# A decoder layer on one core: the first four products of each tile as high, high, low, low

## The chip, the core and the metric

The kernel runs on one core of a Trainium2 chip. Its time is device microseconds of one execution. Before the change it takes 1614.85 us, the median of three runs (1614.5 to 1615.77).

## The reference

One layer of a decoder with 256 tokens and 2048 features, all in float32. A combined projection of the normalised input gives the merge gates and the heads of three token mixers (sparse attention over compressed, selected and recent blocks; stick-breaking attention; attention over keys that an indexer selects). Their outputs are projected, gated, summed and projected once more; then come a gated feed-forward network with a short causal convolution, and a per-layer embedding behind a sigmoid gate. Cut to what matters here:

```python
h = rmsnorm(x, norm_mix)
u = h @ w_in                                  # gates and heads of the three mixers
y = g0 * (o_a @ w_a) + g1 * (o_b @ w_b) + g2 * (o_c @ w_c)
x = x + y @ w_out
h = rmsnorm(x, norm_ffn)
x = x + (gelu(conv(h @ w_gate) + conv_b) * (h @ w_up)) @ w_down
x = x + sigmoid(rmsnorm(x, norm_ple) @ ple_w_gate) * (p @ ple_w_proj)
return rmsnorm(x, norm_final)
```

## The kernel before

Activations are kept with features on the partitions and the 256 tokens along the free dimension. Each float32 operand is split in two rounded parts: a high part, rounded to TensorE's fast float32 format, and a low part, what the rounding left. An activation tile `xs[k]` has 128 features and 512 columns: the high parts of the 256 tokens, then the low parts. A weight block is split in the same way by `split_w` (L114): ScalarE copies the high part (L122), VectorE subtracts it for the low part (L123).

A tile of a matrix product is one block of 128 output features in one PSUM bank of 512 columns. `gemm` (L134) loops over the blocks k of 128 input features. For each it issues two products: the high weights times all 512 columns of `xs[k]` (L140, "a high product"), which leaves high times high in the left half of the bank and high times low in the right half; and the low weights times the 256 high columns alone (L141, "a low product"), added in the right half. `fold` or `add_x` then adds the two halves. Each product loads its own 128 by 128 weights.

`gemm` is called for the feature tiles of the combined projection (35, four of them early, in four pieces of four blocks while the input still arrives), for 48 gate tiles, 48 projections of the mixers (4, 4 or 8 blocks of input), 16 output tiles, 88 tiles of gate and up, and 64 of down (11 blocks). All others have 16 blocks. The weights of a tile come in one or two parts (`parts`), split one after the other; `k0` and `total` say where a piece stands in its tile.

`tile_of` (L216) loads and splits the weights of a tile one tile ahead of the products that use them: the products wait in `pending` until the next tile's load is issued. Attention's small products (`stick`, `index`, `selected`, `sparse`) are generators that `pump` advances by one step between tiles. The value tiles (L328 to L330) and the embedding's gate (L818 to L820) issue their products in threes with other operands, and do not call `gemm`.

The order in which an engine runs its instructions is not quite that of the code. A planner with a simulated timeline orders them when the program is built (`schedule_with_timeline_sim`, L1068), and may put a later instruction ahead of an earlier one that it expects to wait.

Of the kernel before, what the change touches and what calls it, by code (L numbers as in the profile page):

```python
# [38 lines left out]
def trunk(ctx, tc, xT, xtok, pT, wf, wv, wg, wpa, wpb, wpc, wout, ck1, cv1, gmix, params, fg, fu, fd,  # L39
# [12 lines left out]
    mm = nc.tensor.matmul  # L52
# [12 lines left out]
    def feat(name, dt=F32):  # L65
        return f2.tile([P, 512], dt, tag="f2", name=name)
# [18 lines left out]
    for g in range(4):  # L85
        for c in range(2):
            k = 4 * g + 2 * c
# [46 lines left out]
    def gemm(ps, parts, xs, k0=0, total=None):  # L134
        total = total or sum(n for _, _, n in parts)
        k = k0
        for hi, lo, n in parts:
            for j in range(n):
                last = k == total - 1
                mm(ps[:, 0:512], hi[:, j, :], xs[k][:, 0:512], start=k == 0, stop=last)  # L140
                mm(ps[:, 256:512], lo[:, j, :], xs[k][:, 0:256], start=False, stop=last, skip_group_check=True)  # L141
                k += 1

    def fold(dst, ps, name):
        t = tmp("fold")
# [84 lines left out]
    for g in range(4):  # L230
        raw = early_raw[g].rearrange("p (k c) -> p k c", c=128)
        parts = []
        for c in range(2):
            for k in range(4 * g + 2 * c, 4 * g + 2 * c + 2):
                xs = feat("h", F32R)
                act(xs[:, 0:256], x_sb[:, k, :], AF.Copy, scale=gm[:, k:k + 1])
                vec.scalar_tensor_tensor(xs[:, 256:512], x_sb[:, k, :], gm[:, k:k + 1], xs[:, 0:256].bitcast(F32),
                                         op0=ALU.mult, op1=ALU.subtract)
                hs.append(xs)
            parts += split_w(raw[:, 8 * c:8 * c + 8, :], (4, 4) if g == 0 else (8,), 128, g == 0)  # L240
        if g:
            parts = [(hi[:, a:a + 4, :], lo[:, a:a + 4, :], 4) for hi, lo, _ in parts for a in (0, 4)]
        for n in range(EARLY):
            gemm(ps_early[n], parts[n:n + 1], hs, 4 * g, KT)
# [30 lines left out]
    def feature_tiles(n, name, into=None):  # L275
# [27 lines left out]
        def load(parts, i):  # L303
            ps = psg()
            gemm(ps, parts, hs)
            evac(i, ps)
# [368 lines left out]
    def gate_tile(parts):  # L675
        ps = psg()
        gemm(ps, parts, hs)
        gt = tmp("gt")
        fold_norm(gt, ps, norm[0])
        act(gt, gt, AF.Tanh, scale=0.5)  # L680
        latent["gt"] = gt
        pump()
# [58 lines left out]
    xs = []  # L741
# [333 lines left out]
```

## Time and profile before

| what | before |
|---|---|
| median of three runs | 1614.85 us |
| profiled execution | 1616.5 us |
| its span | 1614.7 us |
| PE busy | 1602.2 us (99%) |
| weight loads (PEld) busy | 1403.1 us (87%) |
| VectorE busy | 1136.6 us (70%) |
| ScalarE busy | 869.6 us (54%) |
| HBM traffic over the span | 195 GB/s |

The span is what the profiler saw between the first and the last instruction; the execution's own time is 1.8 us longer. PE is TensorE's matrix product, PEld its weight loads, which overlap the products. A product's duration in a row includes the time until its results are out, and the next product starts before that; so the distance between two starts says what a product costs.

### The profile page before, as it was taken

To read this page: it belongs to the slowest core of one execution; us is meant where nothing else is said; L and a number is where in the kernel's file an instruction comes from. 1 tells how busy PE (TensorE), PEld (TensorE's weight loads), DVE (VectorE), ACT (ScalarE), POOL (GpSimd) and SP (SyncE) were. 2 spreads that over 40 slices of the span, in tenths; PEclk is the share of its full clock that TensorE was granted. 3 is DMA by queue.
4 is the path that set the end of the run, shared out by engine and by line. 5 is a ranking of instruction groups with operands and counts; after the bars stand their busy time and mean duration, and the time that the engine had idled before them with its cause. 6 is when DMAs were issued, how large, how long until landed. Compare 5 with 4: busy or idle time off the path is not lost.

```text
span 1614.7 us, 24245 instructions
## 1 busy us (share of the span) xinstructions
PE 1602.2 (99%) x9186; PEld 1403.1 (87%) x9186; DVE 1136.6 (70%) x1897; ACT 869.6 (54%) x1407; POOL 171.6 (11%) x193
## 2 busy tenths in 40 slices
PE   9999999999999999999999999999999999999997
PEld 8888888888888888888888888888888888888886
DVE  5555857777777666677777777667776677678785
ACT  6585556555555555555655555445544555446554
POOL 0201512100010100022000000000000000002442
PEclk9999999999999999999999999999999999999999
DMA  9854456444445555555555554565546655566862
GB/s 359 286 192 159 166 200 239 169 164 158 164 164 183 193 192 195 209 191 200 184 183 188 199 188 160 178 236 183 186 153 209 209 191 176 164 195 211 278 233 79
DMA packets 57933, 313.39 MB, mean 194 GB/s; under 512 B 6412, under 2 KB 8152, under 8 KB 30040
## 3 DMA queue, kind: packets, MB, share of 16 engines
q1 hardware_dynamic: 54048, 302.05, 53.7%
q0 software_dynamic: 1600, 5.24, 1.0%
q10 hardware_dynamic: 2168, 4.54, 0.9%
q8 instruction: 72, 1.18, 0.3%
q14 instruction: 45, 0.37, 0.1%
HBM read 307.53 MB, written 6.57 MB: 195 GB/s over the span
## 4 chain that ended last, share of the span: by engine, by line
PE 98%; DVE 1%; DMA 0%; ACT 0%; issue 0%; SPq 0%; POOLq 0%; DVEq 0%; ACTq 0%
PE pg L140 56%; PE pg L141 29%; PE pg L818 1%; PE pg L820 1%; PE pg L819 1%; PE pa L820 1%; PE pa L818 1%; PE pa L819 1%; PE pg L329 1%; PE pg L330 1%; PE pg L328 1%; PE po L632 1%; PE po L541 0%; PE po L540 0%; DMA raw<-in_wf_dram 0%; PE pa L589 0%
## 5 line engine op out<-in xcount | busy, mean ns | idle before, releaser
L123 DVE TENSOR_TENSOR lo<-raw,hi 128x1024 fp32r<-128x1024 f32 (+2 forms) x611 | 696.5, 1142 | 371.7 <-ACT hi L122 370.4
L122 ACT ACTIVATE hi<-raw 128x1024 fp32r<-128x1024 f32 (+2 forms) x611 | 598.3, 981 | 644.9 <-PE pg L140 404.9
L140 PE MATMUL pg<-xf,hi 128*128 128x512 f32 x1408 | 488.5, 391 | 0.0
L140 PE MATMUL pg<-h,hi 128*128 128x512 f32 x1300 | 462.4, 397 | 0.2 <-DVE pj L147 0.2
L141 PE MATMUL pg<-xf,lo 128*128 128x256 f32 x1408 | 394.2, 280 | 0.0
L141 PE MATMUL pg<-h,lo 128*128 128x256 f32 x1300 | 366.4, 282 | 0.0
L140 PEld LDWEIGHTS pg<-xf,hi 128*128 128x128 f32 x1408 | 263.3, 187 | 57.7
L140 PEld LDWEIGHTS pg<-h,hi 128*128 128x128 f32 x1300 | 243.6, 188 | 55.7 <-issue 0.7
L141 PEld LDWEIGHTS pg<-xf,lo 128*128 128x128 f32 x1408 | 266.1, 189 | 0.1
L141 PEld LDWEIGHTS pg<-h,lo 128*128 128x128 f32 x1300 | 245.5, 189 | 2.4 <-issue 0.4
L140 PE MATMUL pg<-f,hi 128*128 128x512 f32 x704 | 245.5, 392 | 0.0
L141 PE MATMUL pg<-f,lo 128*128 128x256 f32 x704 | 197.2, 280 | 0.0
L140 PEld LDWEIGHTS pg<-f,hi 128*128 128x128 f32 x704 | 131.7, 187 | 29.4
L141 PEld LDWEIGHTS pg<-f,lo 128*128 128x128 f32 x704 | 133.0, 189 | 0.7
L721 POOL TENSOR_TENSOR ssq<-ssq,sqn 128x256 f32<-128x256 f32 x28 | 32.2, 1151 | 794.6 <-ACT sqn L720 794.6
L140 PE MATMUL pg<-ys,hi 128*128 128x512 f32 x256 | 88.7, 393 | 0.0
L270 POOL TENSOR_TENSOR gt<-fold,r 128x256 f32<-128x256 f32 x48 | 38.3, 799 | 354.2 <-DVE fold L269 281.6
L141 PE MATMUL pg<-ys,lo 128*128 128x256 f32 x256 | 70.8, 277 | 0.0
L140 PEld LDWEIGHTS pg<-ys,hi 128*128 128x128 f32 x256 | 47.9, 187 | 11.0
L146 ACT ACTIVATE fold<-pg 128x256 f32<-128x256 f32 x141 | 51.5, 365 | 6.8 <-PE pg L141 6.8
L141 PEld LDWEIGHTS pg<-ys,lo 128*128 128x128 f32 x256 | 48.1, 188 | 0.1
L140 PE MATMUL pg<-oa,hi 128*128 128x512 f32 x128 | 45.1, 391 | 0.0
(312 smaller groups left out, 1732.2 us busy)
## 6 DMA issues: line engine op xcount, KB each, us to landing
raw<-in_wg_dram SPq DMA_DIRECT2D x48, 1024.0 KB, 4.8
raw<-in_fg_dram SPq DMA_DIRECT2D x44, 1024.0 KB, 4.8
raw<-in_fu_dram SPq DMA_DIRECT2D x44, 1024.0 KB, 4.9
raw<-in_fd_dram SPq DMA_DIRECT2D x64, 704.0 KB, 4.0
raw<-in_wf_dram SPq DMA_DIRECT2D x31, 1024.0 KB, 4.9
raw<-in_wout_dram SPq DMA_DIRECT2D x16, 1024.0 KB, 4.8
raw<-in_plg_dram SPq DMA_DIRECT2D x16, 1024.0 KB, 5.0
raw<-in_wv_dram SPq DMA_DIRECT2D x8, 1024.0 KB, 5.9
```

The source lines that it names most:

```text
L122: act(hi, raw[:, k:k + n, :], AF.Copy)
L123: vec.tensor_tensor(lo, raw[:, k:k + n, :], hi.bitcast(F32), op=ALU.subtract)
L140: mm(ps[:, 0:512], hi[:, j, :], xs[k][:, 0:512], start=k == 0, stop=last)
L141: mm(ps[:, 256:512], lo[:, j, :], xs[k][:, 0:256], start=False, stop=last, skip_group_check=True)
L146: act(t, ps[:, 256:512], AF.Copy)
L270: nc.gpsimd.tensor_tensor(dst, t, r, op=ALU.mult)
L328: mm(pss[t], xh, hi[:, j, :], start=k == 0, stop=False)
L329: mm(pss[t], xl, hi[:, j, :], start=False, stop=False)
L721: (vec if n == KT - 1 else nc.gpsimd).tensor_tensor(ssq, ssq, t, op=ALU.add)
L818: mm(ps, xh, hi, start=first, stop=False)
L819: mm(ps, xl, hi, start=False, stop=False)
L820: mm(ps, xh, lo, start=False, stop=last)
```

## The change

In a piece of a tile that starts at block 0, and only in its first part, the second and the third product change places: high 0, high 1, low 0, low 1, then in turns as before. Which products are issued, their operands and the marks of the first and the last one of a tile stay as they are.

```diff
         for hi, lo, n in parts:
-            for j in range(n):
-                last = k == total - 1
-                mm(ps[:, 0:512], hi[:, j, :], xs[k][:, 0:512], start=k == 0, stop=last)
-                mm(ps[:, 256:512], lo[:, j, :], xs[k][:, 0:256], start=False, stop=last, skip_group_check=True)
-                k += 1
+            order = [(m, j) for j in range(n) for m in (0, 1)]
+            if k == 0:
+                order[1:3] = order[2:0:-1]
+            last = k + n == total
+            for m, j in order:
+                if m == 0:
+                    mm(ps[:, 0:512], hi[:, j, :], xs[k + j][:, 0:512], start=k + j == 0, stop=last and j == n - 1)
+                else:
+                    mm(ps[:, 256:512], lo[:, j, :], xs[k + j][:, 0:256], start=False, stop=last and j == n - 1,
+                       skip_group_check=True)
+            k += n
```

## Rows read from the trace of the kernel before

**Rows 1.** The page: span, busy time of TensorE, shares of the chain that ended last.

```profile
span 1614.7 us, 24245 instructions
...
PE 1602.2 (99%) x9186; PEld 1403.1 (87%) x9186; DVE 1136.6 (70%) x1897; ACT 869.6 (54%) x1407; POOL 171.6 (11%) x193
...
PE 98%; DVE 1%; DMA 0%; ACT 0%; issue 0%; SPq 0%; POOLq 0%; DVEq 0%; ACTq 0%
```

**Rows 2.** DMA issues by tile: count, size, us to landing.

```profile
raw<-in_wg_dram SPq DMA_DIRECT2D x48, 1024.0 KB, 4.8
...
raw<-in_fd_dram SPq DMA_DIRECT2D x64, 704.0 KB, 4.0
raw<-in_wf_dram SPq DMA_DIRECT2D x31, 1024.0 KB, 4.9
```

**Rows 3.** Feed-forward network: high products in 400 us; timeline (start, duration) of neighbours.

```profile
1000.00:1400.00 400.00, 400.00 (x1155) 215.75 (x1155) 1.00 0.56 187
...
600.08 0.39 PE L140 MATMUL pg<-h,hi 128*128 128x512 f32 x1
600.31 0.28 PE L141 MATMUL pg<-h,lo 128*128 128x256 f32 x1
600.43 0.39 PE L140 MATMUL pg<-h,hi 128*128 128x512 f32 x1
```

**Rows 4.** Timeline: first and last of 55 products of 512, then 34 of 256.

```profile
1540.12 0.39 PE L818 MATMUL pa<-hi,xp 128*128 128x512 f32 x1
...
1552.36 0.39 PE L818 MATMUL pa<-hi,xp 128*128 128x512 f32 x1
...
1600.07 0.28 PE L818 MATMUL pg<-hi,xp 128*128 128x256 f32 x1
...
1604.03 0.28 PE L818 MATMUL pg<-hi,xp 128*128 128x256 f32 x1
```

**Rows 5.** Timeline: ends of a run of 77 pairs; then of all 22 runs.

```profile
174.72 0.40 PE L140 MATMUL pg<-h,hi 128*128 128x512 f32 x1
...
201.94 0.40 PE L140 MATMUL pg<-h,hi 128*128 128x512 f32 x1
...
78.45 0.40 PE L140 MATMUL pg<-h,hi 128*128 128x512 f32 x1
...
1516.12 0.40 PE L140 MATMUL pg<-f,hi 128*128 128x512 f32 x1
```

**Rows 6.** Timeline around 692 us (x2: two neighbours of one line).

```profile
691.60 0.63 PE L140 MATMUL pg<-ys,hi 128*128 128x512 f32 x2
692.07 0.40 PE L141 MATMUL pg<-ys,lo 128*128 128x256 f32 x2
692.31 0.40 PE L140 MATMUL pg<-ys,hi 128*128 128x512 f32 x1
```

**Rows 7.** Timeline: ends of six products at 16 us; two highs at 260 us.

```profile
16.04 0.63 PE L140 MATMUL pg<-h,hi 128*128 128x512 f32 x2
...
17.08 0.40 PE L140 MATMUL pg<-h,hi 128*128 128x512 f32 x1
...
260.02 0.63 PE L140 MATMUL pg<-h,hi 128*128 128x512 f32 x2
...
260.60 0.40 PE L140 MATMUL pg<-h,hi 128*128 128x512 f32 x1
...
261.66 0.40 PE L140 MATMUL pg<-h,hi 128*128 128x512 f32 x1
```

**Rows 8.** Timeline: the second early tile's first products.

```profile
8.98 0.50 PE L140 MATMUL pg<-h,khi 128*128 128x512 f32 x1 [1.28 <-ACT khi L122]
9.70 0.43 PE L141 MATMUL pg<-h,klo 128*128 128x256 f32 x1 [0.23 <-DVE klo L123]
9.93 0.63 PE L140 MATMUL pg<-h,khi 128*128 128x512 f32 x1
10.36 0.42 PE L141 MATMUL pg<-h,klo 128*128 128x256 f32 x1
```

## The prediction

> **What bounds the kernel now.** I read the page first, then the TensorE rows in order of time. The page says that nothing but TensorE counts: the chain that ended last lies 98% on PE, and PE is busy 1602.2 of 1614.7 us [rows 1]. A busy share says little here, because a product shows as busy until it has drained, so I looked at the distances between the starts of neighbouring products instead.
>
> In the feed-forward network a tile is a strict alternation: a high product of 512 columns, a low one of 256, the next high. High to low takes 0.23 us, low to high 0.12 us, a pair 0.35 us [rows 3]. The long stretch gives the pair more sharply: 1155 high products in 400 us, so 0.3463 us, and up to 0.3466 us if the product cut by the edge is left out [rows 3]. No product waits for weights, for PSUM or for a splitting engine there: the next tile's first product keeps the same step. So a change of order on TensorE is not hidden by anything: each nanosecond per tile is on the path.
>
> Two other rows say what a product pays beside its columns. Where all products have 512 columns, 54 of them take 12.24 us, 0.2267 us each; where all have 256, 33 take 3.96 us, 0.1200 us each [rows 4]. Doubling the columns adds 0.1067 us, which leaves 0.0133 us per product that doesn't depend on its width. A pair priced so is 0.2267 + 0.1200 = 0.3467 us, the pair of the feed-forward network. I call this the fast rhythm.
>
> There is a second one. Between 174.72 and 201.94 us, in the same code, 77 pairs take 27.22 us, 0.3535 us each [rows 5]: three pairs in 1.06 us where the fast rhythm takes 1.04 us. Nothing waits there either. Counted over the trace, six or more such pairs in a row occur 22 times, the first from 78.45, the last up to 1516.12 us, 474 pairs in all [rows 5]. They stand in the stages in which attention's small products cut in, and among the embedding products; from 520 to 1460 us there is none. So the stream settles in one of two rhythms, keeps it across tile boundaries, and changes it when something breaks the alternation. That is what the change does, once in each tile.
>
> **The change, part by part.** Added and removed: no product, no weight load, no evacuation and no DMA. Moved: in each tile whose count starts at zero, the second high product goes ahead of the first low one. SP's and POOL's queues are not touched.
>
> How many tiles: 35 feature tiles (31 with a load of their own and the four early ones), 48 gate tiles, 48 projections, 16 output tiles, 88 of gate and up, 64 of down: 299. The load counts agree [rows 2].
>
> The four products by themselves: before, three distances high-low, low-high, high-low; after, high-high, high-low, low-low. High-high and low-low are 0.2267 and 0.1200 us from the rows of equal width [rows 4], together 0.3467 us, and what they replace is 0.3467 us [rows 3]. By these rows the edit costs nothing.
>
> But the trace holds this very order, since the planner that orders the instructions has put it there: at 691.60 us two high products follow one another, at 692.07 two low ones, and the next high starts at 692.31 [rows 6]. That is 0.705 us from the unrounded starts (0.71 by the rows) where two pairs of the fast rhythm take 0.6933. So one such group cost 0.012 us more than turns, and the stream went on at 0.3467 us a pair afterwards. Another place has high, high, low, high, low, low at 16.04 us, and the next high at 17.08 [rows 7]: 1.047 us unrounded against 1.040 for three fast pairs, so 0.007 us; the same six recur six times up to 33 us. Upper end: 299 x 0.012 = 3.5 us, lower end of what such groups show: 299 x 0.007 = 2.1 us. Against three pairs of the slow rhythm (1.06 us) the second row is 0.013 us less, so below nothing the bound is what the slow stretches cost now: 474 x 0.0067 = 3.2 us, if each tile's start threw the stream into the fast rhythm. I take 0.012 us, since that group has the same four products in a stage like the one where most tiles stand: +3.5 us.
>
> [...]
>
> The start: the second early tile's first high product starts at 8.98, its first low one waits for the low half of the weights until 9.70, PE idle for 0.23 us, the next high follows at 9.93 and its low at 10.36 [rows 8]. After the change the second high product runs inside that wait. A high product takes 0.43 us there (9.93 to 10.36, twice its share at full speed: the lower of the clock's two levels, 1.2 and 2.4 GHz, after PE had stood still for 1.28 us). Gain at most 0.4 us, and half of it if the clock rises at the same moment as now; for this I take -0.3 us. At the very first tile all four products have their data, so nothing changes there. Should the cover be missing, the low product is late by one high product, +0.4 us.
>
> The added wait: the third product instead of the second now waits for the tile's low weights. Behind it stand only the tile's own products, and in the steady stages the unbroken step shows that the low weights are there.
>
> Sum: +3.5 - 0.3 = +3.2 us. On the profiled execution (1616.5 us, its span 1614.7 and 1.8 around it) this gives 1619.7; that execution lies 1.65 us above the median of the runs, 1614.85, so the forecast for the median is 1618.0 us, with a range of its own from 1616.6 (2.1 per 299 tiles, less the start) to 1621.
>
> **The rivals.** Second case: the stream locks into the slow rhythm in the feed-forward network. For it: two high products in a row at 260.02 us, after which three pairs from 260.60 to 261.66 take 1.06 us [rows 7], although the pairs before were fast; and the groups at 16 to 33 us never leave the slow rhythm. Against it: the group at 691.60 did not do that. Price: from the output projection on there are 2368 pairs in 168 tiles (16 x 16 + 88 x 16 + 64 x 11); without the two of each group 2032, x 0.0067 = 13.6 us; the earlier 131 tiles have 1584 pairs (83 x 16, 32 x 4, 16 x 8), 1322 without the groups, x 0.0067 = 8.9 us, of which 3.2 are paid already. Together 1614.85 + 13.6 + 5.7 - 0.3 = 1634; if half of the tiles lock, 1624. It decides as soon as the group leaves a tile in the slow rhythm and the next group doesn't lift it out.
>
> Third case: the order costs nothing, each product pays its columns and its constant, and the rhythms stay where they are: 1614.85 - 0.3 = 1614.6. For it: equal-width rows. Against it: the two measured groups. The planner may also put the old order back here and there, which ends in the same place.
>
> Fourth case, on the other side: the group resets the stream to the fast rhythm in the mixed stages, and costs nothing itself where it is fast already: 1614.85 - 3.2 - 0.3 = 1611.3. For it: a break has often ended a slow stretch. Against it: it needs both halves; with the group's own 0.007 us it ends at 1613.4, no change.
>
> Fifth: the planner moves attention's small products. The stream then changes rhythm elsewhere, within the bounds given.
>
> **How the numbers follow.** First case 0.40, second 0.25, third 0.22, fourth 0.10, fifth 0.03. What a measurement can tell from no change is 0.2%, 3.2 us: below 1611.6 faster, above 1618.1 slower. The first case straddles the upper bound, about half on each side. Faster: most of the fourth case and a little of the fifth, 0.10. Slower: half of the first, nearly all of the second and a little of the fifth, 0.46. Same: 0.44. The range runs from 1612.5 (leaving out most of the fourth case) to 1628 (leaving out the locked half of the second), 1612.5 to 1628.
>
> **What would show it.** In the changed kernel's TensorE rows: at a tile's start high, high, low, low, and from the first high to the fifth product 0.705 us (first case), 0.693 (third). Then the pairs: 0.3467 us between 1000 and 1400 us confirms the first or third case, three pairs in 1.06 us the second; pairs of 0.3467 us between 174 and 202 us speak for the fourth. At 9 us the wait for the low half should show no idle PE. I am wrong if the pair in the feed-forward network is anything but 0.3467 us, or if PE shows new idle time at tile starts.

## The result: 1627.8 us, slower by 13.1 us

The changed kernel takes 1627.83 us, the median of four runs (1627.6 to 1628.24); the kernel before takes 1614.72 beside it (1614.5 to 1615.77). The ratio is 1.008, with an interval from 1.0063 to 1.0098. The time lies inside the range by 0.2 us at its upper end, on the side to which 0.46 was given (no change: 0.44). The likeliest case, 1618.0, is missed by 9.8 us: what happened is the second case.

The page of the changed kernel, against [rows 1]: the chain is as before, and PE is busy 11.8 us longer in a span that is 11.4 us longer.

```profile
span 1626.1 us, 24245 instructions
...
PE 1614.0 (99%) x9186; PEld 1401.8 (86%) x9186; DVE 1138.8 (70%) x1897; ACT 869.3 (53%) x1407; POOL 171.8 (11%) x193
...
PE 98%; DVE 1%; DMA 0%; ACT 0%; issue 0%; SPq 0%; POOLq 0%; DVEq 0%; ACTq 0%
```

Where the time went is read from two starts in the timeline of the changed kernel (start, duration): the first product of the output projection, and the last high product of the down tiles; ahead of them stands the last product of the value tiles.

```profile
222.15 0.39 PE L336 MATMUL pg<-lo,h 128*128 128x512 f32 x1
...
682.68 0.40 PE L144 MATMUL pg<-ys,hi 128*128 128x512 f32 x1
...
1527.50 0.40 PE L144 MATMUL pg<-f,hi 128*128 128x512 f32 x1
```

Before, the same three (the last of them is in [rows 5], at 1516.12):

```profile
224.12 0.39 PE L330 MATMUL pg<-lo,h 128*128 128x512 f32 x1
...
682.93 0.39 PE L140 MATMUL pg<-ys,hi 128*128 128x512 f32 x1
```

So the stretch from the output projection to the down tiles grew from 833.19 to 844.82 us, by 11.6 of the 13.1 us. Ahead of it, from the last value product to the output projection, 458.82 us became 460.53: 1.7 more. Up to the last value product the changed kernel is 2.0 us earlier. That is no gain of the change: in the profiled execution of before the second early weight block landed 1.3 us later, and then the granted clock fell to half (window, its length, PE busy with the count of products, granted clock, DMA share, GB/s):

```profile
10.00:13.00 3.00, 3.00 (x11) 0.50 1.02 383
```

In the other twelve profiled executions the clock is full in this window and 18 to 20 products start in it.

The high products in windows (window, its length, PE busy with the count of products, the same of the weight loads, granted clock, DMA share, GB/s): 1138 where [rows 3] has 1155, at the same full clock (a few records can be missing). From 525 to 682 us 451, where the kernel before, in the second fence, has 454.

```profile
525.00:682.00 157.00, 154.31 (x451) 81.59 (x450) 1.00 0.55 199
...
1000.00:1400.00 400.00, 394.23 (x1138) 208.10 (x1137) 1.00 0.55 183
```

```profile
525.00:682.00 157.00, 157.00 (x454) 84.71 (x453) 1.00 0.54 198
```

That the busy time is below 400 us is no idle time of PE: the window is of the high products alone, and in each group two low ones run between the second high and the third. A tile's start in the feed-forward network of the changed kernel (start, duration; x2 are two neighbours of one line) answers to [rows 6]:

```profile
1004.34 0.40 PE L144 MATMUL pg<-xf,hi 128*128 128x512 f32 x1
...
1004.69 0.40 PE L144 MATMUL pg<-xf,hi 128*128 128x512 f32 x1
...
1005.05 0.62 PE L144 MATMUL pg<-xf,hi 128*128 128x512 f32 x2
1005.51 0.40 PE L146 MATMUL pg<-xf,lo 128*128 128x256 f32 x2
1005.75 0.40 PE L144 MATMUL pg<-xf,hi 128*128 128x512 f32 x1
...
1006.10 0.40 PE L144 MATMUL pg<-xf,hi 128*128 128x512 f32 x1
...
1006.46 0.40 PE L144 MATMUL pg<-xf,hi 128*128 128x512 f32 x1
1006.69 0.28 PE L146 MATMUL pg<-xf,lo 128*128 128x256 f32 x1
1006.81 0.40 PE L144 MATMUL pg<-xf,hi 128*128 128x512 f32 x1
```

The group takes 0.70 us (1005.05 to 1005.75), where two fast pairs take 0.693. The pairs on both sides of it are the news: three take 1.06 us (1005.75 to 1006.81), the slow rhythm of [rows 5].

Read from the unrounded starts of the 283 groups whose products stand right behind one another, the stream has three patterns, and the group moves it between them:

| pattern | its pairs, ns | mean | group met in it | pattern behind |
|---|---|---|---|---|
| A, fast and even | 346 and 347 | 346.7 | 705 ns | B |
| B, fast and uneven | 350, 343 in turns | 346.7 | 692 to 696 ns | C, always |
| C, slow, met behind its long pair | 350, 361, 349 in turns | 353.3 | 695 ns | C (106 of 106 that could be read) |
| C, slow, met behind its third pair | the same | 353.3 | 696 to 697 ns | B |

Two fast pairs are 693.3 ns, so a group costs 2 ns where most groups stand. The cost lies in the 14 pairs between one group and the next: a slow tile takes 695 + 14 x 353.3 = 5642 ns against 5547. With 16 blocks, 14 pairs behind the group, the tile ends on the long pair and the next group leaves it in C. A down tile has 9 pairs behind its group, ends on the third pair, and the next tile is fast, in B; the group behind that one makes C again. Of the tiles from 682 us on whose pairs could be read without a gap, 98 of 99 with 14 pairs are slow, and 27 of 55 with 9: 1615 pairs x 6.67 ns = 10.8 us, and 168 groups x 2 to 3 ns give 0.4; measured 11.6. The 14 tiles that something interrupts are not in this sum.

### The profile page after: what moved, and what is told of

Its sections match the earlier page's. It is cut to its first block, busy times and chain, and to the rows that moved or that the text cites. A ratio compares the mean times of both kernels' runs of the same rounds, so it can differ in the third digit from the quotient of the medians.

```text
span 1626.1 us, 24245 instructions
## 1 busy us (share of the span) xinstructions
PE 1614.0 (99%) x9186; PEld 1401.8 (86%) x9186; DVE 1138.8 (70%) x1897; ACT 869.3 (53%) x1407; POOL 171.8 (11%) x193
## 4 chain that ended last, share of the span: by engine, by line
PE 98%; DVE 1%; DMA 0%; ACT 0%; SPq 0%; issue 0%; POOLq 0%; DVEq 0%; ACTq 0%
PE pg L144 56%; PE pg L146 28%; PE pg L824 1%; PE pg L826 1%; PE pg L825 1%; PE pa L824 1%; PE pa L825 1%; PE pa L826 1%; PE pg L336 1%; PE pg L334 1%; PE pg L335 1%; PE po L638 1%; DMA raw<-in_wf_dram 0%; PE po L547 0%; PE po L546 0%; PE pa L595 0%
## 5 line engine op out<-in xcount | busy, mean ns | idle before, releaser
L146 PE MATMUL pg<-xf,lo 128*128 128x256 f32 x1408 | 380.9, 281 | 0.0
L146 PE MATMUL pg<-h,lo 128*128 128x256 f32 x1300 | 352.7, 281 | 0.5 <-DVE lo L123 0.5
L144 PEld LDWEIGHTS pg<-xf,hi 128*128 128x128 f32 x1408 | 258.8, 188 | 57.5
L144 PEld LDWEIGHTS pg<-h,hi 128*128 128x128 f32 x1300 | 238.7, 188 | 51.2 <-issue 1.1
L146 PE MATMUL pg<-f,lo 128*128 128x256 f32 x704 | 186.3, 279 | 0.0
L144 PEld LDWEIGHTS pg<-f,hi 128*128 128x128 f32 x704 | 127.8, 188 | 26.2
```

Of the source, the lines that this page charges most:

```text
L144: mm(ps[:, 0:512], hi[:, j, :], xs[k + j][:, 0:512], start=k + j == 0, stop=last and j == n - 1)
L146: mm(ps[:, 256:512], lo[:, j, :], xs[k + j][:, 0:256], start=False, stop=last and j == n - 1, skip_group_check=True)
```

## The experiments

In all of them a product order is edited at chosen blocks alone: `gemm` gets a list `at` of blocks, and at block a the low product of a and the high one of a + 1 change places. The comparison is with the runs of the kernel before on the same chip, whose median over all was 1614.4 to 1614.8.

**One group in the whole kernel**, at the start of the third gate tile of the feed-forward network.

```diff
-        gemm(ps, parts, xs)
+        gemm(ps, parts, xs, at=(0,) if f == 2 else ())
```

> One group high, high, low, low in a single tile (gate tile 2 of the feed-forward network), all other tiles in turns. Theory 'rhythm': the changed kernel's trace shows that a group met in the even fast rhythm (346/347 ns a pair) takes 705 ns instead of 693 and leaves the stream in the other fast one (350, 343 in turns), so the pairs after it still average 346.67 ns: +0.01 us, same time as before (1614.7). Rival 'each group pays for itself': +0.01 us, the same. Rival 'the pair is slower in a tile that starts so': at most 14 x 7 ns = 0.1 us, also the same. This run alone tells nothing apart; it is the base for the next two.

Measured 1614.07 us, ratio 0.9996 (0.9986 to 1.0005): no change.

**Two groups**, the same and one at the start of the up tile that follows it.

> Two groups: gate tile 2 and the up tile right behind it, 2 tiles of 299; nothing else. Rhythm: the second group meets the 350, 343 rhythm and leaves the slow one (three pairs in 1060 ns), which nothing breaks until the embedding's products at about 1462 us: some 1920 pairs x 6.67 ns = +12.8 us, so 1627.5 us. Each group pays for itself: +0.02 us. The pair is slower in a tile that starts so: +0.2 us at most. So 1627.5 against 1614.7 to 1614.9.

Measured 1627.09 us, ratio 1.0079 (1.0062 to 1.0096): two swaps in a kernel of 9186 products cost nearly all that the change costs. The timeline of this kernel at the first group, then at the second:

```profile
792.40 0.63 PE L146 MATMUL pg<-xf,hi 128*128 128x512 f32 x2
792.86 0.40 PE L148 MATMUL pg<-xf,lo 128*128 128x256 f32 x2
793.10 0.40 PE L146 MATMUL pg<-xf,hi 128*128 128x512 f32 x1
793.34 0.28 PE L148 MATMUL pg<-xf,lo 128*128 128x256 f32 x1
793.45 0.39 PE L146 MATMUL pg<-xf,hi 128*128 128x512 f32 x1
...
797.96 0.63 PE L146 MATMUL pg<-xf,hi 128*128 128x512 f32 x2
798.42 0.40 PE L148 MATMUL pg<-xf,lo 128*128 128x256 f32 x2
798.65 0.40 PE L146 MATMUL pg<-xf,hi 128*128 128x512 f32 x1
...
799.00 0.40 PE L146 MATMUL pg<-xf,hi 128*128 128x512 f32 x1
...
799.37 0.40 PE L146 MATMUL pg<-xf,hi 128*128 128x512 f32 x1
...
799.71 0.40 PE L146 MATMUL pg<-xf,hi 128*128 128x512 f32 x1
```

The first group takes 0.70 us (792.40 to 793.10) and leaves a pair of 0.35; behind the second three pairs take 1.06 us (798.65 to 799.71). From there 1908 pairs in a row are slow: 1908 x 6.67 ns = 12.7 us, against 12.3 measured. The window of [rows 3] in this kernel has the slow count, 400 us / 0.3533 = 1132:

```profile
1000.00:1400.00 400.00, 400.00 (x1133) 212.74 (x1133) 1.00 0.56 184
```

**Three groups**: a third one, five blocks behind the second, should undo it.

```diff
-        gemm(ps, parts, xs, at=(0,) if f == 2 else ())
+        gemm(ps, parts, xs, at=(0, 5) if f == 2 else ())
```

> Three groups: as the run with two, and one more in the same up tile, at blocks 5 and 6, three pairs behind the second group. Rhythm: in the changed kernel a group that meets the slow rhythm after nine pairs (a whole number of its three-pair turns, the last pair 349 or 350 ns) leaves the 350, 343 rhythm; after three pairs the same holds, so the third group undoes the second: +0.03 us, 1614.8 us. Each group pays for itself: +0.04 us. A theory in which what a group does adds up would give more than the run with two.

Measured 1614.41 us, ratio 0.9999 (0.999 to 1.0008). The third group stands behind three slow pairs, and the window is the one of before:

```profile
1000.00:1400.00 400.00, 400.00 (x1155) 216.33 (x1154) 1.00 0.57 187
```

So one swap more is worth 12.7 us less: it is not the swap that costs, but the pattern that it leaves.

**The group in the later tiles alone**: the 168 tiles of output projection, gate, up and down, `at=(0,)` in their four calls.

> The group at the start of all tiles of the output projection and the feed-forward network (168 tiles), in turns in the 131 tiles before. Rhythm: this is where the changed kernel lost: its tiles there start 0.2 us earlier than before's (682.7 against 682.9 us) and end 11.4 us later; so +11.6 us, 1626.3 us. Each group pays for itself (12 ns): +2.0 us, 1616.7. If the planner's moves in the stages before were the cause: 1614.7.

Measured 1626.38 us, ratio 1.0073 (1.0058 to 1.0088).

**The group in the earlier tiles alone**: the four early tiles, 31 feature tiles, 48 gate tiles and 48 projections.

> The group only at the starts of the tiles ahead of the output projection (four early tiles, 31 feature tiles, 48 gate tiles, 48 projections); the 168 tiles from 682 us on in turns. Theory (a break decides the rhythm of what follows, and the loss is made in the feed-forward network): the changed kernel's 1627.8 less the 1626.4 of the kernel with the group in the later tiles alone, so 1.45 us over the before, 1616.1, and pairs of 0.3467 us between 1000 and 1400 us in a run whose stream arrives there in the fast even rhythm. If each group costs 0.012 us whatever follows: 131 x 0.012 - 0.3 = +1.3, 1615.9, with the pairs before 520 us unchanged. If the groups lock the mixed stages as they lock the later ones: +5.7 us, 1620. If they lift slow stretches: 1611.4 to 1614.

Measured 1616.39 us, ratio 1.0013 (1.0004 to 1.0022). The two halves are 11.6 and 2.0 us over the before, together 13.6 against 13.1 of the whole. The window from 1000 to 1400 us has its 1155 high products again, so nothing of the earlier tiles is carried into the later ones; from 525 to 682 us it has 451:

```profile
525.00:682.00 157.00, 154.31 (x451) 81.62 (x450) 1.00 0.55 198
...
1000.00:1400.00 400.00, 400.00 (x1155) 215.91 (x1154) 1.00 0.57 187
```

There, 372 pairs take 349.6 ns in the mean instead of 346.7, 1.1 us, and 39 groups 0.1. The loss that shows lies behind the value tiles: from their last product to the output projection this kernel takes 460.5 us, and ten executions with the order of before there take 458.5 to 458.8.

**How many pairs stand between groups**: gate and up tiles with two groups each, with 3 pairs between them and 9 behind, and the other way round.

```diff
-        gemm(ps, parts, xs)
+        gemm(ps, parts, xs, at=(0, 5))
```

The other kernel has `at=(0, 11)`.

> Two groups in each of the 88 gate and up tiles, at blocks 0 and 5 (three pairs between them, nine behind), in turns elsewhere. Rhythm: the first group meets the 350, 343 rhythm and leaves the slow one, the second meets it after its third pair and leaves the 350, 343 one: 692.5 + 1060 + 696.5 + 9 x 346.67 = 5569 ns a tile against 5547 in turns, 88 x 0.022 = +2.0 us, 1616.7; the down tiles between stay fast. Each group or each tile start pays for itself: twice the groups of a kernel with one per tile, so at least as slow as that (88 x 95 ns = +8.4 us and more, over 1623).

> As turn39, but the second group at block 11: nine pairs between the groups, three behind. Same number of groups, same products. Rhythm: nine pairs run slow and three fast: 692.5 + 9 x 353.33 + 696.5 + 3 x 346.67 = 5609 ns, 88 x 0.062 = +5.5 us, 1620.2. Each group pays for itself: the same time as turn39.

Measured 1617.03 us, ratio 1.0015 (1.0006 to 1.0024), and 1620.39 us, ratio 1.0036 (1.0022 to 1.0049). Both have the same 176 groups; they differ in which stretch of a tile is slow. 88 tiles x 6 pairs x 6.67 ns = 3.5 us; measured 3.4. The window in the first kernel, then in the second:

```profile
1000.00:1400.00 400.00, 393.43 (x1151) 209.34 (x1151) 1.00 0.57 187
```

```profile
1000.00:1400.00 400.00, 393.36 (x1146) 208.30 (x1145) 1.00 0.57 185
```

**High, high, low, low throughout**: the swap at every second block of every tile.

> High, high, low, low in all tiles from the first to the last block (an odd last block in turns). Rhythm: the trace shows no group right behind another, so this asks what the chip settles in; bounds per group 693.3 ns (columns and constant alone; with the slow stretches gone as well 1614.7 - 3.9 = 1610.8 us) and 705 ns (some 1980 groups x 11.7 ns = +23 us, 1638). Each group pays for itself, at the 695 ns that most groups of the changed kernel took: +3.3 us, 1618.

Measured 1616.96 us, ratio 1.0015 (1.0006 to 1.0024). Most groups take 696 to 698 ns (start, duration):

```profile
1099.85 0.63 PE L146 MATMUL pg<-xf,hi 128*128 128x512 f32 x2
1100.32 0.40 PE L148 MATMUL pg<-xf,lo 128*128 128x256 f32 x2
1100.55 0.63 PE L146 MATMUL pg<-xf,hi 128*128 128x512 f32 x2
...
1102.64 0.62 PE L146 MATMUL pg<-xf,hi 128*128 128x512 f32 x2
```

Four groups take 2.79 us (1099.85 to 1102.64), 0.697 each. That is 3.7 ns more than two fast pairs and 9.7 less than two slow ones. From the output projection to the down tiles this kernel takes 837.0 us against 833.2, 3.8 more; the whole is only 2.3 over the before. That the earlier stages give back the rest because their slow stretches are gone is not shown: in this kernel the planner also moved 362 of the 1282 products outside `gemm`. Two swaps cost 12.3 us, a swap everywhere 2.3.

**The early tiles alone.**

> The group only in the four early tiles. Theory: the second high product runs while the low half of the weights is still being made, so the second early tile's wait at 9 us goes and the time falls by 0.3 us, to 1614.3; the first early product of the second round (16.04 us in the profiled execution of before) comes earlier by that against the end of the second block's load. Rival: the wait is that of a transfer that ends last anyway, 1614.6 and the second round no earlier.

Measured 1614.6 us, ratio 1.0001 (0.9993 to 1.001): no gain is seen, though an interval from -1.1 to +1.6 us can't exclude 0.3. The timeline of this kernel, at the second early block and at the end of the early tiles (in brackets, idle time before and what ended it):

```profile
8.36 0.50 PE L148 MATMUL pg<-h,klo 128*128 128x256 f32 x2
...
12.96 0.28 PE L148 MATMUL pa<-h,klo 128*128 128x256 f32 x1
13.58 0.73 PE L146 MATMUL pg<-h,hi 128*128 128x512 f32 x2 [0.34 <-ACT hi L122]
14.84 0.39 PE L148 MATMUL pg<-h,lo 128*128 128x256 f32 x1 [0.53 <-DVE lo L123]
```

The low product at 8.36 has no idle time before it, as forecast for [rows 8]. But the early tiles then end sooner, and the next tile's first product waits 0.34 us for its high weights and its low one 0.53 us for the other half. In the kernel with one group, whose early tiles are in turns, the last early product starts at 13.27 instead of 12.96, and the next tile starts at the same time and waits the same:

```profile
13.27 0.28 PE L148 MATMUL pa<-h,klo 128*128 128x256 f32 x1
13.60 0.73 PE L146 MATMUL pg<-h,hi 128*128 128x512 f32 x2
14.86 0.38 PE L148 MATMUL pg<-h,lo 128*128 128x256 f32 x1 [0.52 <-DVE lo L123]
```

In both kernels ScalarE starts the split of that tile as soon as its block has landed, at the same time, first in this kernel, then in the one with one group:

```profile
12.46 1.06 ACT L122 ACTIVATE hi<-raw 128x1024 fp32r<-128x1024 f32 x1 [0.98 <-DMA raw<-in_wf_dram]
```

```profile
12.48 1.06 ACT L122 ACTIVATE hi<-raw 128x1024 fp32r<-128x1024 f32 x1 [1.10 <-DMA raw<-in_wf_dram]
```

So the rival fits these two executions: a transfer ends last, and the products ahead of it gain nothing. It is two executions alone. Over twelve profiled executions (all but that of before) this tile starts between 13.2 and 14.2 us, which scatters more than the 0.3 us in question.

**A group used to leave the slow pattern**: one group in each of three long slow stretches of before, in feature tile 17, feature tile 22 and the last down tiles; then without tile 17.

```diff
-            gemm(ps, parts, hs)
+            gemm(ps, parts, hs, at={17: (0,), 22: (5,)}.get(at, ()))
...
-        gemm(ps, parts, fts)
+        gemm(ps, parts, fts, at=(2,) if last and n == 12 else ())
```

> Three groups in all, each right behind a full turn of the slow rhythm in one of the three longest slow stretches of the kernel before: feature tile 17 at block 0, feature tile 22 at block 5, down tile 12 of the last chunk at block 2; in turns elsewhere. Rhythm: the rest of the three stretches, 47, 74 and 41 pairs, runs in the 350, 343 rhythm: -162 x 6.67 ns = -1.1 us, 1613.6 us. Each group pays for itself: +0.01 to +0.04 us, 1614.7. In the trace the pairs from 140 to 155, 175 to 200 and 1500 to 1514 us take 346.67 ns instead of 353.33.

Measured 1613.80 us, ratio 0.9995 (0.9986 to 1.0004). Two groups did what they should. The one in tile 17 met pattern B, not C, and left C behind:

```profile
139.21 0.39 PE L146 MATMUL pg<-h,hi 128*128 128x512 f32 x1
...
139.55 0.62 PE L146 MATMUL pg<-h,hi 128*128 128x512 f32 x2
140.02 0.40 PE L148 MATMUL pg<-h,lo 128*128 128x256 f32 x2
140.25 0.40 PE L146 MATMUL pg<-h,hi 128*128 128x512 f32 x1
...
140.60 0.40 PE L146 MATMUL pg<-h,hi 128*128 128x512 f32 x1
...
140.96 0.40 PE L146 MATMUL pg<-h,hi 128*128 128x512 f32 x1
...
141.31 0.40 PE L146 MATMUL pg<-h,hi 128*128 128x512 f32 x1
```

> As the kernel with a group in each of three slow stretches, without the one in feature tile 17. There the stretch at 138 us was slow in three of eight profiled executions of the same order and fast in the others, so a group there can only help in some; without it an execution that arrives fast stays fast. Theory: the two other groups end their stretches (175 to 200 us and 1500 to 1513 us at 0.3467 us a pair), the stretch at 138 us falls either way: 1613.6 to 1613.9. If a group helps nowhere: 1614.6.

Measured 1613.81 us, ratio 0.9996 (0.9987 to 1.0005). (The text on record counts three of eight executions that were slow at 138 us; it is four of eight.) In the profiled execution of this kernel the 72 pairs from 175.35 to 200.31 us take 0.3467 us each; [rows 5] has 0.3535 there.

```profile
175.35 0.40 PE L146 MATMUL pg<-h,hi 128*128 128x512 f32 x1
...
200.31 0.40 PE L146 MATMUL pg<-h,hi 128*128 128x512 f32 x1
```

The two stretches hold 115 slow pairs, 0.77 us; measured 0.8 and 0.6. That these two kernels beat the one before is likely by the trace, and not shown by the times.

## Why the prediction was right and wrong

**The range:** that the time lies in it is luck. Its upper end, 1628, came from leaving out the locked half of the second case, and what happened is the second case with nearly all of the later gate and up tiles locked; the sum of the first case, +3.2 us, is not what the runs show.

**What bounds the kernel, and the two rhythms:** right as far as it went. TensorE alone counts, the fast and the slow pair are what decides, and the price of 6.7 ns per slow pair came out within 0.5 us in every kernel for which it is reckoned in full above. (Slow stretches of six or more pairs occur 28 times before, with 517 pairs; 22 times and some 475 pairs is what runs of eight or more give. The six products at 16.04 us recur at 21.67 and 27.31 alone; in three more places up to 33 us three more pairs stand between. The row at 600 us in [rows 3] is of the mixers' projections, not of the feed-forward network, as the text has it; its pair is the same.)

**The step that failed** is "So one such group cost 0.012 us more than turns, and the stream went on at 0.3467 us a pair afterwards", and with it the term 299 x 0.012. Both halves are true of the group at 691.60, which met pattern A: the kernel with one group shows the same 705 ns and the same 346.7 behind it. The error was to multiply it by 299. The first group leaves the stream in B, with the same mean, so the mean that I read couldn't tell A from B; the second group meets B, and leaves it for C. In the changed kernel 134 groups of 283 take 695 ns and 13 take 705. So the group costs 2 ns instead of 12, and the pairs behind it in the later tiles, which I took for unchanged, cost 11 us. The trace of before showed A and B apart in its unrounded starts: ahead of the group at 691.60 the pairs are 346 and 347 ns, behind it 350 and 343 in turns.

**The second case** had the mechanism and its condition, "as soon as the group leaves a tile in the slow rhythm and the next group doesn't lift it out". Its price of 13.6 us for the later tiles is 2.0 too high against the 11.6 measured, because half of the down tiles are lifted out: their 9 pairs against 14 decide it, which no row of before could tell. For the earlier tiles 5.7 us were priced and 2.0 measured. I gave this case 0.25, with the row at 260.02 us [rows 7] for it and the group at 691.60 against it. The two rows do not contradict each other: the group at 691.60 met A, and the two highs at 260.02 met B, since the four pairs ahead of them are 351, 344, 350 and 342 ns. The row at 260 is not the same group, as no two lows follow, but it showed what two highs do to a stream in B.

**The start:** the wait at 9 us went, as forecast, but no run shows the -0.3 us. I had priced a wait without asking what is late next: in the kernel with the early tiles alone, the next tile's weights were late by as much. The price was also read in an execution that is not typical. A high product took 0.43 us there at a granted clock of 0.50; that half clock, in none of the other twelve profiled executions, goes with the 1.65 us by which the profiled execution lay above the median.

**The third case** (the order costs nothing): refuted for the whole, true of a single group. Its ground was the rows of equal width. No price by columns and a constant alone can give both 346.7 and 353.3 ns for the same two products at the same granted clock. The Trainium skill, "TensorE: Matmul & The Clock Gate", section "Back-to-back issue gap", gives such a price, N / 2.4 + 2.5 ns, for an isolated product, and says that in a stream the weight loads count too. The rows here disagree with that price: 226.7 and 120.0 ns are each 11 ns more.

**The fourth case** (the group lifts the mixed stages): refuted, the earlier tiles alone lose 2.0 us. The group can lift a slow stretch, where it is set at the right pair, but not at each tile's start.

**The fifth case** (the planner): refuted. All 1282 products outside `gemm` stand in the same order, 1274 of them behind the same number of products of `gemm`, 8 one product later.

## What to carry to other kernels

In a stream of unequal products, the distance between two starts can depend on the order of products long before; look for several means of one pattern in the trace, and list what was before and behind each change of mean, before a single row is multiplied by a count. A break that costs nothing once may cost on the second time; count how many products stand between breaks, since that decides where the next one leads. When a wait at the start goes, look for the next one before it is booked as gain.

## What the runs showed of the hardware

The same two products, each with its own weights, keep to 346.7 or 353.3 ns a pair for up to 1908 pairs on end, and neither waits nor the clock differ. One swap of neighbours takes the stream from one to the other. What in TensorE holds that pattern was not shown; every product here loads its own weights, and no run changed that, so the part of the loads is open.

After a stage of attention's small products the pattern is not the same in every execution: of ten profiled executions with the order of before at that place, the stretch from 137 us on (53 pairs) was slow in four. Another, from 30 us on (56 or 60 pairs), was slow in four, three of them executions in which the first was fast. Such a stretch is worth 0.35 to 0.4 us, so a part of the spread of the runs of before (1613.55 to 1615.26 in 27) may come from there; that is not shown.
